# A transformer step on eight cores: softmax arithmetic reordered in every tile, and the first tile's weight loads, stores and constants rearranged

## The chip, the cores and the metric

The kernel runs on the eight cores of one Trainium2 chip, the same program on each core. The metric is the device time of the slowest core, in microseconds (us).

An execution falls into one of two states. In the fast one all cores agree within a fraction of a per cent. In the slow one cores of one die, or of both, get a lower TensorE clock for a part of the run or all of it, and the run is some per cent longer.

In the profiles PE is TensorE (PEld its weight loads), DVE is VectorE, ACT is ScalarE, POOL is GpSimd, and SP is SyncE, which here only issues transfers. L284 is line 284 of the kernel that ran; most operations go through helpers, so the same helper has another line number before and after.

## The reference

One encoder layer over 16 prompts of 4096 rows (65,536 rows of width 1024, so two prompts for each core), and over 16 short continuations of 16 rows (32 "sample rows" for each core):

```python
h = rms_norm(x, n_pre_mix)
q, k, v, zg, ga, gb = split(h @ w_in)
a = attn_prompt(q, k, v, sinks)          # 64-row chunks see themselves and two chunks before
u, gv = split(gelu(zg)); gv = layer_norm(gv, ln_g, ln_b)
bm = spatial_gate(u, gv, w_s, b_s)       # 128x128 lower-triangular mix
merged = sigmoid(ga) * (a @ w_attn_proj) + sigmoid(gb) * (bm @ w_gmlp_proj)
x = x + rms_norm(merged @ w_out, n_post_mix)
g, up = split(rms_norm(x, n_pre_ffn) @ w_ffn_in)
x = x + rms_norm((silu(g) * up) @ w_ffn_out, n_post_ffn)

# inside the attention: a softmax whose denominator has one more term for each head
denom = sum(p) + exp(sinks - m)
p = p / denom
```

Inputs, weights and outputs are f32.

## The kernel before

Each core works through 16 tiles of 512 rows; the 32 sample rows go along in tile 0. The weights are 34 blocks of up to 1 MB in bf16. They don't stay on the core: a ring of eight 1 MB slots is refilled all the time. In tile 0 a block is read as f32 by a converting DMA (on the POOL queue), in one, two or four pieces, and the bf16 result is stored to a scratch copy in HBM (on the SP queue). From tile 1 on, the SP queue reads the bf16 copy. This function keeps the ring filled:

```python
def pump():
    while W["issue"] < len(wseq) and W["free"]:
        ...                                        # next block `key`, slot s
        if key in W["seen"]:                       # later tiles: bf16 from scratch
            m.dma(SP, ("ring", s), ring[:, s, 0:nkc, :], view[key], reads=[("scr", key)], writes=RK(s))
            continue
        W["seen"].add(key)
        q = key[0] == "win" and key[1] < 2         # the two q blocks need a second slot
        g = W["free"].pop(0) if q else s
        for idx, src in f32_pieces(key):           # every piece writes RK(g): each waits for the last
            m.dma(POOL, ("ringc", g), ring[:, g][idx], src, writes=RK(g))
        if q:
            ...                                    # two DVE copies that lay the heads out anew
        m.dma(SP, ("cvst", key), view[key], ring[:, s, 0:nkc, :], reads=RK(s), writes=[("scr", key)])
```

Attention goes through eight pairs (of a 128-row block and two key heads) in a tile. `S(n)` makes the scores of pair n and their exponentials. `PV(n)` multiplies by the values (the first 256 columns of a bank) and by ones (the other 256, the sums), and ends with the division:

```python
def S(n):
    for c in range(2): ...      # score products on 64x128 tiles of the PE array
    for c in range(2): ...      # score products on 64x64 tiles
    act(PT[...], ..., AF.Exp); act(PT3[...], ..., AF.Exp)

def PV(n):
    ...                         # products with V (128x64, then 64x64) and with ones
    act(od, ps[:, 4:6, :], AF.Copy, B(4, 5), ok_)          # values and sums out of PSUM
    eng = DVE if FIRST[0] or n == 7 else POOL
    tt(eng, d4, d4, esb, ALU.add, ...)                     # + exp(sink)
    recip(od[:, :, 256:512], od[:, :, 256:512], ok_, ok_)  # on DVE
    tt(eng, ao, o4, d4, ALU.mult, ...)                     # into aT, bf16

for n in range(7):
    PV(n); S(n + 1); g_unit(2 * n + 2); g_unit(2 * n + 3)
    if n < 6: spatial(*sp[n + 2])
```

The start, and the sample rows' four rounds of attention at the end of mixing:

```python
for bl in range(4):                      # rows of x: statistics, scale, transpose
    ...
SM.load(); SM.norm(0)                    # sample rows
for u in qkv_units(tiles[0]): u()        # q, then k, then v
setup_rest()                             # gains, sinks, spatial weights: loads and preparation
SM.caches()
...
for n in range(4 if i0 else 0):          # at the end of tile 0's mixing
    SM.S(n); SM.PV(n)
```

The softmax here doesn't subtract the row's maximum and nothing guards it: scores larger than these inputs give would overflow.

Of the kernel before, what the change touches and what calls it, by code (L numbers as in the profile page):

```python
# [6 lines left out]
F32 = mybir.dt.float32  # L7
# [185 lines left out]
def build_program(n_prompt_tiles=16, do_sample=True):  # L193
# [34 lines left out]
    with ExitStack() as st:  # L228
# [18 lines left out]
        dent = sb("dent", [128, 2, 512], F32)  # L247
        hst = sb("hst", [128, 2, D], BF16)
        gvn = mgT.rearrange("p (s a) n -> p s (a n)", s=4)
# [24 lines left out]
        mgTs = sb("mgTs", [128, 8, 32], BF16)  # L274
        actTs = sb("actTs", [128, 22, 32], BF16)
        ps = st.enter_context(nc.psum_tensor("ps", [128, 8, 512], F32))
# [71 lines left out]
        FIRST = [True]  # L348
        PX = lambda: DVE if FIRST[0] else POOL

# [46 lines left out]
        wseq = list(QKV_KEYS)  # L397
# [7 lines left out]
        W = dict(issue=0, use=0, free=list(range(SLOTS)), where={}, seen=set())  # L405
# [3 lines left out]
        def pump():  # L409
            while W["issue"] < len(wseq) and W["free"]:  # L410
                u = W["issue"]
                key = wseq[u]
                s = W["free"].pop(0)
                W["where"][u] = s
                W["issue"] += 1
                nkc = view[key].shape[1]
                if key in W["seen"]:
                    m.dma(SP, ("ring", s), ring[:, s, 0:nkc, :], view[key], reads=[("scr", key)], writes=RK(s))
                    continue
                W["seen"].add(key)  # L420
                q = key[0] == "win" and key[1] < 2
                g = W["free"].pop(0) if q else s
                for idx, src in f32_pieces(key):
                    m.dma(POOL, ("ringc", g), ring[:, g][idx], src, writes=RK(g))
                if q:
                    d5 = ring[:, s].rearrange("p k (g h d) -> p k h g d", g=4, h=2)
                    s5 = ring[:, g].rearrange("p k (h g d) -> p k h g d", g=4, h=2)
                    for hh in range(2):
                        copy(DVE, d5[:, :, hh], s5[:, :, hh], RK(g), RK(s))
                    W["free"].append(g)  # L430
                m.dma(SP, ("cvst", key), view[key], ring[:, s, 0:nkc, :], reads=RK(s), writes=[("scr", key)])

        def wget(key):
            u = W["use"]
            assert wseq[u] == key, (u, wseq[u], key)
            pump()
            assert W["issue"] > u, ("no ring slot", key)
            W["use"] += 1
            s = W["where"].pop(u)
            return ring[:, s], ("ring", s), s  # L440
# [5 lines left out]
        def rsqrt(P, c, eps):  # L446

            o, i_ = stt[0:P, c + 1:c + 2], stt[0:P, c:c + 1]
            if FIRST[0]:
                ts(DVE, o, i_, float(eps), None, ALU.add, None, SK(c), SK(c + 1))  # L450
                act(o, o, AF.Sqrt, SK(c + 1), SK(c + 1))
                recip(o, o, SK(c + 1), SK(c + 1))
            else:
                ts(POOL, o, i_, float(eps), None, ALU.add, None, SK(c), SK(c + 1))
                tt(POOL, o, o, negh[0:P, 0:1], ALU.pow, SK(c + 1) + ["negh"], SK(c + 1))
# [17 lines left out]
        class PostNorm:  # L473
# [12 lines left out]
            def apply(self):  # L486
# [5 lines left out]
                if self.dst is None:  # L492
                    tt(DVE, self.x, self.x, tf, ALU.add, self.tk + self.xk, self.xk)
                else:
                    tt(PX(), tf, self.x, tf, ALU.add, self.tk + self.xk, self.tk)
                    q = ACT if FIRST[0] else POOL
                    m.dma(q, ("yst", self.ti, q), self.dst, tf, reads=self.tk)
# [9 lines left out]
        def scale_gamma(eng, i):  # L507
            ts(eng, gS[:, i, :], gS[:, i, :], 32.0, None, ALU.mult, None, [("gS", i)], [("gS", i)])

        load_gamma(0)  # L510
        m.op(POOL, lambda e: e.memset(negh[:], -0.5), writes=["negh"])
        m.op(POOL, lambda e: e.memset(ones[:], 1.0), writes=["ones"])
        t0_, t0k = tmp1()
        m.op(POOL, lambda e: e.memset(t0_[:, 0:128], 1.0), writes=t0k)
        m.op(POOL, lambda e: e.affine_select(out=t0_[:, 0:128], in_=t0_[:, 0:128], pattern=[[-1, 128]],
                                             compare_op=ALU.is_equal, fill=0.0, base=0, channel_multiplier=1),
             reads=t0k, writes=t0k)
        copy(DVE, ident[:], t0_[:, 0:128], t0k, ["ident"])
        scale_gamma(DVE, 0)
        pump()  # L520

        def setup_rest():
            for i in (1, 2, 3):
                load_gamma(i)
            m.dma(ACT, "c_lng", lng[:], ln_g[0:1, :].partition_broadcast(128), writes=["lng"])
            m.dma(ACT, "c_lnb", lnb[:], ln_b[0:1, :].partition_broadcast(128), writes=["lnb"])
            m.dma(ACT, "c_es", es[:], sinks[0:1, :].partition_broadcast(128), writes=["es"])
            for i in (1, 2, 3):
                scale_gamma(POOL, i)
            act(es[:], es[:], AF.Exp, ["es"], ["es"])  # L530
            for tp in range(2):
                for hf in range(2):
                    copy(DVE, es2[64 * hf:64 * hf + 64, 4 * tp:4 * tp + 4],
                         es[64 * hf:64 * hf + 64, 4 * (2 * tp + hf):4 * (2 * tp + hf) + 4], ["es"], ["es2"])
            a, ak = tmp1()
            wv = a.rearrange("p (g s) -> p g s", g=4)
            m.dma(ACT, "c_ws", wv, w_s.rearrange("g t s -> t g s"), writes=ak)
            m.op(POOL, lambda e: e.affine_select(out=wv, in_=wv, pattern=[[0, 4], [-1, 128]], compare_op=ALU.is_ge,
                                                 fill=0.0, base=0, channel_multiplier=1), reads=ak, writes=ak)
            wb = hst[:, 0, 0:512]  # L540
            copy(DVE, wb, a, ak, [("hst", 0)])
            for g in range(4):
                tp_(pTv[:, g * 128:(g + 1) * 128], wb[:, g * 128:(g + 1) * 128], ident[:], [("hst", 0)])
            copy(DVE, WmT[:].rearrange("p g t -> p (g t)"), pTv[:, 0:512], B(TB), ["WmT"])
            c, ck_ = tmp1()
            m.dma(ACT, "c_bs", c[0:1, :], b_s[0:1, :], writes=ck_)
            m.op(POOL, lambda e: e.memset(bsb[:], 0.0), writes=["bsb"])
            copy(DVE, bsb[0:1].rearrange("p g t -> p (g t)"), c[0:1, :], ck_ + ["bsb"], ["bsb"])
            if not do_sample:
                return  # L550
            d, dk = tmp1()
            wv2 = d[0:32, 0:128].rearrange("p (g s) -> p g s", g=4)
            m.op(POOL, lambda e: e.memset(d[0:32, 0:128], 0.0), writes=dk)
            for s in range(2):
                m.dma(ACT, "c_ws2", wv2[16 * s:16 * s + 16, :, 16 * s:16 * s + 16],
                      w_s[:, 0:16, 0:16].rearrange("g t s -> t g s"), writes=dk)
            m.op(POOL, lambda e: e.affine_select(out=wv2, in_=wv2, pattern=[[0, 4], [-1, 32]], compare_op=ALU.is_ge,
                                                 fill=0.0, base=0, channel_multiplier=1), reads=dk, writes=dk)
            wb2 = hst[0:32, 1, 0:128]
            copy(DVE, wb2, d[0:32, 0:128], dk, [("hst", 1)])  # L560
            for g in range(4):
                tp_(pTv[0:32, g * 32:(g + 1) * 32], wb2[:, g * 32:(g + 1) * 32], ident[0:32, 0:32], [("hst", 1)])
# [3 lines left out]
            m.op(POOL, lambda e: e.memset(msk[:], 1.0), writes=["msk"])  # L566
            for s, (base, cm) in enumerate(((15, -1), (-16, 1))):
                m.op(POOL, (lambda s, base, cm: lambda e: e.affine_select(
                    out=msk[:, s, :], in_=msk[:, s, :], pattern=[[0, 64]], compare_op=ALU.is_ge, fill=0.0, base=base,
                    channel_multiplier=cm))(s, base, cm), reads=["msk"], writes=["msk"])  # L570
# [12 lines left out]

        class Sample:
            KH = ["hTs"]
            x = gx[0:32, 1, :]
            XK = [("gx", 1)]

            def load(self):
                m.dma(ACT, "xs", self.x, xs[:, :], writes=self.XK)  # L590

            def norm(self, gi):
                r = nstats(32, self.x, self.XK, 0)
                nscale(32, self.x, self.XK, gi, r, 0)
                ntrans(32, 0, hTs[:], ["hTs"])
# [7 lines left out]
            def kv(self, w):  # L603
# [10 lines left out]
                for s in range(2):  # L614
                    m.dma(ACT, uniq("so"), ks[s, 112:128, :], t[16 * s:16 * s + 16, 0:256], reads=tk)
                    m.dma(ACT, uniq("so"), vs[s, 112:128, :], t[16 * s:16 * s + 16, 256:512], reads=tk)
                for src_c, dst_c in ((ck, ks), (cv, vs)):
                    m.dma(ACT, uniq("so"), dst_c[:, 0:112, :], src_c[:, 16:128, :])

            def caches(self):  # L620
                for s in range(2):
                    t, tk = tmp1()
                    m.dma(ACT, ("ckl", s), t[:, 0:256], ck[s], writes=tk)
                    m.dma(ACT, ("ckl", s), t[:, 256:512], cv[s], writes=tk)
                    copy(DVE, hst[:, s, 0:256], t[:, 0:256], tk, [("hst", s)])
                    copy(DVE, Vc[:, s, :], t[:, 256:512], tk, [("Vc", s)])
                    for j in range(2):
                        tp_(pTv[:, j * 128:(j + 1) * 128], hst[:, s, j * 128:(j + 1) * 128], ident[:], [("hst", s)])
# [666 lines left out]
```

## Time and profile before

| | before |
|---|---|
| first three runs | 4425.69, 4432.07, 5141.29 us (the last one slow) |
| profiled run, fast | 4423.02 us; spans of the cores 4407.2 to 4421.5, clock 0.976 to 0.979 |
| tile 0 with its start (median of the eight cores) | 545.7 us |
| a later tile | some 257.9 us (257 to 259), PE busy in 252.5 to 254 of them |

The slices, stretches and timelines (start, duration, engine, line, operation, and in brackets the idle time before it and what ended it) of this profile are quoted in the prediction. Each later tile begins with a load of the Gelu table on ACT, and I use the first such row after tile 0 as the end of tile 0. On the slowest core, core 3, in the timeline of ACT (start, duration, engine, line, operation, and in brackets the idle time before it and what ended it):

```profile
552.56 1.28 ACT L293 ACT_TABLE_LOAD   x1 [10.17 <-DMA ys<-gx]
```

PE's waits in the later tiles (view of waits, 1000 to 4200 us; columns: total us, times, longest) are led by the attention blocks and the spatial product:

```profile
PE ps L284 <- DVE aT L303: 24.6, 12, 2.1
PE ps L284 <- DVE big L303: 17.3, 26, 1.2
PE ps L284 <- POOL aT L303: 5.4, 12, 0.7
```

`aT` is the divided attention output: it comes late once a tile, by 2.1 us. `big` holds what the spatial products feed.

In tile 0 (the same core, 0 to 555 us) PE's three largest waits are far longer. The first is for copies of the constants and of the sample rows' caches (one of them 56.3 us), the second for normed rows, the third for banks that ACT frees:

```profile
PE ps L288 <- DVE hst L300: 71.5, 4, 56.3
PE ps L288 <- DVE hst L314: 62.1, 6, 29.9
PE ps L284 <- ACT big L293: 36.2, 4, 27.7
```

### The profile page before, as it was taken

The page shows a single profiled execution, that of the slowest core. Times are in us where ns is not written, and L with a number is a line of the kernel's source. Part 1 is how long each engine was busy: PE and PEld are TensorE (multiplying, and loading weights), DVE is VectorE, ACT ScalarE, POOL GpSimd, SP SyncE. Part 2 cuts the span into 40 slices and gives each one's busy share as a digit, 9 for nine tenths or more (in the row PEclk, how much of TensorE's full clock was granted, in tenths as well). Part 3 has the DMA queues.
Part 4 walks back from the last instruction along what each step waited for, and adds up shares of the span by engine and source line. Part 5 has one row for each costly group of instructions (what it writes and reads, how often), then busy time and mean ns, then how long its engine had stood idle before and what let it go on. Part 6 is the DMA issues. An engine that isn't in the chain of part 4 may idle for free.

```text
span 4421.5 us, 60878 instructions; the slowest of 8 cores (4407.2 to 4421.5 us)
## 1 busy us (share of the span) xinstructions
PE 4125.1 (93%) x23024; PEld 1929.8 (44%) x23024; DVE 1789.7 (40%) x1784; ACT 1386.2 (31%) x2151; POOL 802.2 (18%) x1023
## 2 busy tenths in 40 slices
PE   2569899999999999999999999999999999999988
PEld 1234344444444444444444444444444444444443
DVE  1343162443516244361634436162443616244351
ACT  1333142422414242241424224142422414242231
POOL 0101020302212030221203022120302212030211
PEclk9779999999999999999999999999999999999999
DMA  9659944545345454534545453454545345454532
GB/s 201 120 119 176 242 140 149 184 146 196 135 140 180 153 181 145 194 134 145 181 148 181 150 190 133 147 181 149 184 146 191 136 143 181 148 185 149 188 105 81
DMA packets 154876, 705.20 MB, mean 159 GB/s; under 512 B 13205, under 2 KB 59861, under 8 KB 89046
## 3 DMA queue, kind: packets, MB, share of 16 engines
q1 hardware_dynamic: 96192, 627.09, 41.3%
q0 software_dynamic: 55216, 67.12, 8.2%
q10 hardware_dynamic: 3182, 7.10, 0.6%
q8 instruction: 190, 3.11, 0.3%
q14 instruction: 96, 0.79, 0.1%
HBM read 666.85 MB, written 69.99 MB: 167 GB/s over the span
## 4 chain that ended last, share of the span: by engine, by line
PE 72%; DVE 10%; POOL 6%; DMA 5%; issue 4%; ACT 2%; ACTq 0%; another core or an unknown queue 0%; POOLq 0%; DVEq 0%; SPq 0%
PE ps L284 70%; DVE tmp L318 7%; POOL tmp L303 3%; POOL aT L303 2%; PE ps L288 1%; ACT tmp L293 1%; DMA yp<-tmp 1%; DVE tmp L314 1%; DMA ring<-wap 1%; DMA es<-sinks 1%; DVE hst L314 1%; DVE tmp L303 1%; POOL stt L303 1%; DMA ring<-w_in 1%; DMA ring<-wout 0%
## 5 line engine op out<-in xcount | busy, mean ns | idle before, releaser
L284 PE MATMUL ps<-aT,ring 128*128 128x512 bf16 x6656 | 1473.9, 381 | 36.2 <-DVE aT L303 28.7
L293 ACT ACTIVATE tmp<-ps 128x512 f32<-128x512 f32 (+2 forms) x620 | 475.5, 767 | 1835.8 <-PE ps L284 1660.3
L284 PE MATMUL ps<-hT,ring 128*128 128x512 bf16 x4352 | 999.9, 381 | 28.3 <-DVE big L303 20.9
L284 PEld LDWEIGHTS ps<-aT,ring 128*128 128x128 bf16 x6656 | 649.0, 98 | 817.2 <-issue 58.1
L303 DVE TENSOR_TENSOR big<-ps,tmp 128x512 bf16<-128x512 f32 x352 | 243.5, 692 | 985.3 <-PE ps L284 937.5
L284 PEld LDWEIGHTS ps<-hT,ring 128*128 128x128 bf16 x4352 | 410.9, 98 | 529.9 <-issue 58.3
L284 PE MATMUL ps<-ring,big 128*128 128x512 bf16 x2816 | 612.8, 380 | 8.2 <-DMA ring<-wfo 8.2
L307 POOL TENSOR_SCALAR stt<-stt 128x1 f32<-128x1 f32 x296 | 130.0, 439 | 2522.1 <-ACT tmp L293 2040.9
L318 DVE RECIPROCAL tmp<-tmp 128x512 f32<-128x512 f32 x128 | 429.2, 3353 | 244.4 <-POOL tmp L303 242.1
L314 DVE SCALAR_TENSOR_TENSOR tmp<-ps,stt,gS 128x1024 f32<-128x1024 f32 x129 | 165.6, 1284 | 766.0 <-POOL stt L303 732.5
L284 PEld LDWEIGHTS ps<-ring,big 128*128 128x128 bf16 x2816 | 275.4, 98 | 342.6 <-issue 12.4
L293 ACT ACTIVATE big<-ps 128x512 bf16<-128x512 f32 x384 | 229.6, 600 | 268.3 <-PE ps L284 268.3
L284 PE MATMUL ps<-ring,hT 128*128 128x512 bf16 (+1 forms) x1536 | 301.9, 349 | 7.5 <-DVE tmp L314 3.8
L284 PE MATMUL ps<-big,ring 128*128 128x512 bf16 x1024 | 237.2, 382 | 0.5 <-DVE tmp L314 0.5
L284 PE MATMUL ps<-ring,mgT 128*128 128x512 bf16 x1024 | 229.0, 379 | 2.0 <-DVE tmp L314 1.0
L288 PE MATMUL ps<-ident,hst 128*128 128x128 bf16 (+1 forms) x1052 | 87.2, 230 | 145.9 <-DVE hst L300 71.5
L284 PEld LDWEIGHTS ps<-ring,hT 128*128 128x128 bf16 x1536 | 150.3, 99 | 146.0 <-issue 20.7
L303 POOL TENSOR_TENSOR aT<-tmp 128x512 bf16<-128x512 f32 x105 | 144.8, 1379 | 378.5 <-DVE tmp L318 346.1
L293 ACT ACTIVATE PT<-ps 128x512 bf16<-128x512 f32 (+2 forms) x264 | 193.3, 790 | 13.8 <-PE ps L284 13.6
L314 DVE SCALAR_TENSOR_TENSOR tmp<-big,ps 128x1024 f32<-128x1024 bf16 x128 | 156.2, 1220 | 98.8 <-PE ps L284 97.8
L293 ACT ACTIVATE hT<-ps 128x1024 bf16<-128x1024 bf16 x64 | 65.6, 1025 | 395.3 <-PE ps L288 395.3
L303 POOL TENSOR_TENSOR stt<-stt,negh 128x1 f32<-128x1 f32 x296 | 170.6, 576 | 44.8 <-POOL stt L307 1.3
(125 smaller groups left out, 2559.8 us busy)
## 6 DMA issues: line engine op xcount, KB each, us to landing
ring<-s_win SPq DMA_DIRECT2D x165, 1024.0 KB, 5.5
ring<-s_wfi SPq DMA_DIRECT2D x165, 1024.0 KB, 5.3
ring<-s_wfo SPq DMA_DIRECT2D x60, 1024.0 KB, 5.5
xt<-xp SPq DMA_DIRECT2D x64, 512.0 KB, 5.1
gx<-xp SPq DMA_DIRECT2D x60, 512.0 KB, 5.4
ring<-s_wgp SPq DMA_DIRECT2D x30, 1024.0 KB, 12.7
ring<-s_wap SPq DMA_DIRECT2D x30, 1024.0 KB, 10.8
ring<-s_wout SPq DMA_DIRECT2D x30, 1024.0 KB, 5.0
```

Of the source, the lines that this page charges most:

```text
L284: m.op(PE, lambda e: e.matmul(out, lhsT=lhsT, rhs=rhs, start=start, stop=stop, skip_group_check=True), reads=reads, writes=[("ps", bank)])
L288: m.op(PE, lambda e: e.transpose(out=out, in_=in_, identity=idn), reads=reads + ["ident"], writes=[("ps", TB)])
L293: m.op(ACT, lambda e: e.activation(out=out, in_=in_, func=func, scale=scale, **kw), reads=reads, writes=writes)
L303: m.op(eng, lambda e: e.tensor_tensor(out=out, in0=in0, in1=in1, op=op), reads=reads, writes=writes)
L307: m.op(eng, lambda e: e.tensor_scalar(out=out, in0=in0, scalar1=s1, scalar2=None, op0=op0), reads=reads, writes=writes)
L314: m.op(DVE, lambda e: e.scalar_tensor_tensor(out=out, in0=in0, scalar=scalar, in1=in1, op0=op0, op1=op1), reads=reads, writes=writes)
L318: m.op(DVE, lambda e: e.reciprocal(out=out, in_=in_), reads=reads, writes=writes)
```

## The change

It has two aims. In every tile, POOL should not wait for DVE's reciprocal in place. In tile 0, loads, stores, constants and sample rows should not wait for one another in sequence. The core of the diff, cut:

```diff
 # every tile: the end of PV, and the order in S
-                eng = DVE if FIRST[0] or n == 7 else POOL
-                tt(eng, d4, d4, esb, ALU.add, ok_ + ["es2"], ok_)
+                tt(POOL, d4, d4, esb, ALU.add, ok_ + ["es2"], ok_)
+                if mults:
+                    mults.pop()(POOL)
                 recip(od[:, :, 256:512], od[:, :, 256:512], ok_, ok_)
-                tt(eng, ao, o4, d4, ALU.mult, ok_, [("aT", 4 * tp + g) for g in range(4)])
+                mults.append(lambda eng: tt(eng, ao, o4, d4, ALU.mult, ok_, [("aT", 4 * tp + g) for g in range(4)]))
+                if n == 7:
+                    mults.pop()(DVE)
 # (cut: in S the 64x64 score products now come before the 64x128 ones)

 # tile 0: stores spread over three tiles, pieces of a block not behind one another
+            if key not in STORE:
+                STORE[key] = 0 if key in QKV_KEYS else len(STORE) % 3
...
+                f32 = turn <= STORE[key]
...
-                for idx, src in f32_pieces(key):
-                    m.dma(POOL, ("ringc", g), ring[:, g][idx], src, writes=RK(g))
+                    for k, (idx, src) in enumerate(f32_pieces(key)):
+                        m.dma(POOL, ("ringc", g), ring[:, g][idx], src, writes=[] if k else RK(g))
 # (cut: the store is issued when the block is first used; k and v are projected before q)

 # tile 0: the start
+        first_stats(0)
+        first_stats(1)
+        pump(1)
+        first_stats(2)
+        first_rows(0)
+        first_stats(3)
+        pump(1)
...
+        pump()
+        const_loads()
         for u in qkv_units(tiles[0]):
             u()
-        setup_rest()
 # (cut: constants prepared among the gate projections; gains 1 to 3 loaded later; sample rows in
 #  buffers of their own, one attention round in place of four; outputs of tiles 0 to 2 stored by SP;
 #  the norms' and divisions' arithmetic of tile 0 on POOL, where before it was on DVE and ACT)
```

## The prediction

> **What bounds the kernel now.** I read the table of cores first (spans of 4407.2 to 4421.5 us, clocks of 0.976 to 0.979: no slow die), then the slices of the page, then busy times by stretch, then the instruction timeline of one later tile and of the start. The slices and the queue rows of the page:
>
> ```profile
> PE 4125.1 (93%) x23024; PEld 1929.8 (44%) x23024; DVE 1789.7 (40%) x1784; ACT 1386.2 (31%) x2151; POOL 802.2 (18%) x1023
> PE   2569899999999999999999999999999999999988
> PEclk9779999999999999999999999999999999999999
> DMA  9659944545345454534545453454545345454532
> ```
>
> A slice is 110.5 us. PE (TensorE) is the bound everywhere except in the first five slices. There, and only there, DMA is at 9 tenths, PE is low and the granted clock falls. So there are two questions: what the first tile of 512 rows costs, and what keeps a later tile from being PE alone. Busy time by stretch (us and instruction count of PE, PEld, DVE, ACT, POOL; then clock, DMA share, GB/s), tile 0 with its start first, two later tiles, then pieces of tile 0:
>
> ```profile
> 0.00:554.60 554.60, 353.82 (x2481) 174.08 (x2481) 169.90 (x262) 139.63 (x239) 54.33 (x69) 0.86 0.83 172
> 885.80:1143.70 257.90, 252.46 (x1384) 117.74 (x1384) 108.87 (x103) 84.22 (x129) 50.03 (x64) 1.00 0.47 162
> 2690.20:2948.10 257.90, 253.79 (x1385) 118.68 (x1384) 108.39 (x103) 84.09 (x129) 50.12 (x64) 0.99 0.46 161
> 93.00:160.00 67.00, 3.24 (x17) 1.60 (x18) 4.31 (x17) 1.50 (x2) 10.70 (x10) 0.50 0.80 176
> 235.00:320.00 85.00, 45.80 (x376) 23.88 (x375) 33.24 (x47) 25.19 (x43) 1.91 (x3) 0.72 0.47 116
> 400.00:447.00 47.00, 47.00 (x389) 23.91 (x388) 9.77 (x19) 8.52 (x18) 6.99 (x8) 1.00 1.04 195
> ```
>
> Tile 0 ends at 554.6 us; every later one takes 257.9 us, of which PE is busy some 253.3 and idle 4.6. From 93 to 160 us PE does nothing, and from 235 to 320 us both PE and DMA are half idle: tile 0 is not bound by one resource but by orders of waiting. From 400 to 447 us DMA is saturated (1.04). The rows that name the waits, from the timeline of the start:
>
> ```profile
> 58.08 9.48 PE L284 MATMUL ps<-hT,ring 128*128 128x512 bf16 x32
> 118.65 8.28 POOL L307 TENSOR_SCALAR gS<-gS 128x1024 f32<-128x1024 f32 x3 [32.00 <-DMA gS<-g]
> 132.23 1.28 ACT L293 ACT_TABLE_LOAD   x1 [55.80 <-DMA es<-sinks]
> 192.48 0.61 POOL L136 DMA_DIRECT2D ring<-wap  x1 [5.49 <-DMA ring<-wap]
> 320.14 0.87 POOL L136 DMA_DIRECT2D ring<-wfi  x1 [83.00 <-PE ps L284]
> ```
>
> The first projection starts only at 58 us. Then constants that mixing needs (gains, sinks, spatial weights) are fetched behind a full weight queue and hold ACT for 55.8 us. POOL issues the pieces of one weight block one after the other, each waiting for the last. And no weight load is issued for 83 us while PE works through sample rows.
>
> A later tile, its attention part:
>
> ```profile
> 2651.09 1.03 POOL L303 TENSOR_TENSOR tmp<-tmp,es 128x512 f32<-128x512 f32 x1
> 2652.23 3.35 DVE L318 RECIPROCAL tmp<-tmp 128x512 f32<-128x512 f32 x1 [1.96 <-POOL tmp L303]
> 2655.72 1.27 POOL L303 TENSOR_TENSOR aT<-tmp 128x512 bf16<-128x512 f32 x1 [3.60 <-DVE tmp L318]
> 2656.95 1.04 POOL L303 TENSOR_TENSOR tmp<-tmp,es 128x512 f32<-128x512 f32 x1
> 2680.64 1.89 PE L284 MATMUL ps<-hT,ring 128*128 128x512 bf16 x8 [1.16 <-DVE big L303]
> 2693.89 1.16 PE L284 MATMUL ps<-aT,ring 128*128 128x512 bf16 x4 [2.05 <-DVE aT L303]
> ```
>
> POOL adds, waits 3.60 us for DVE's reciprocal, multiplies, and only then adds for the next pair: a loop of 2656.95 - 2651.09 = 5.86 us. PE's work per pair is 5.46 us (it starts a pair's value product at 2648.08, 2653.54, 2659.00). So POOL's loop falls behind by 0.4 us a pair, and more where two statistics come between; PE then waits on the spatial product's bank (1.16 us) and at the end on the last attention block (2.05 us).
>
> **What the Trainium skill says.** "TensorEngine Tiling (Array Packing)", Tiling Modes, has that a change of tiling mode drains TensorE. The trace agrees: a gap of 0.20 us in weight loads at each change from 128x64 to 64x64 to 64x128 and back. "DMA: Bandwidth & Descriptors", SWDGE vs HWDGE vs iDMA, has that a cast during a DMA can only be issued from GpSimd; here all f32 weight loads are in fact on POOL, and all 1 MB bf16 stores and reloads on SP. "HBM Reference", Specifications, gives about 358 GB/s for each core where both of a pair stream. In the page's own counts (of 2-byte results) the first 100 us moved 196 GB/s at a share over 1; no run here shows the limit itself. "TensorE: Matmul & The Clock Gate", Part 1, has half clock after an idle window; the trace agrees (0.50 from 93 to 160 us).
>
> **The change, part by part.**
>
> (1) Later tiles. POOL's multiply for pair n-1 is put behind the add for pair n, so POOL no longer waits for the reciprocal in place; the last add goes from DVE to POOL. POOL then has 1.04 + 1.26 = 2.3 us per pair, and 3.2 us where a statistic comes between, DVE 3.35 + 0.63 = 4.0 us, ACT up to 5.0 us: all under PE's 5.46. For the end of attention, counted from the start T of the last value product: copy done at T+2.15, add at T+3.35, reciprocal T+6.8, multiply T+7.5. PE by then has 0.9 us of value product, 5.35 of gate product and 2.7 of the first half of the attention projection, so needs the block only at T+9.0. In the trace of before it came at T+11.3. So I expect the whole 4.6 us of idle time to go. Half of the score products are moved next to the value products of the same 64x64 mode: one drain fewer, about 0.12 us, times 7 = 0.85 us. The tiles at clock 0.99 are 1.3 us busier than those at 1.00; with no gaps some of that should go: 0.3 us. Sum 5.7 us a tile, times 15 = 86 us.
>
> (2) Tile 0. POOL's software queue no longer serializes pieces; each block's store to scratch is spread over tiles 0, 1 and 2 (14, 10 and 10 of 34 blocks), the others being read again in f32; constants are fetched before the projections; gains 1 to 3 later; k and v come first, which need one ring slot and no re-layout; sample rows are put among other work with their own buffers, and four sample attention rounds become one.
> PE's need: one steady tile's 253 us, 28 us for the first projections (58.08 to some 86 us in the trace), about 41 us for the remaining sample products (84 of 512 columns at 0.216 us, some 750 of 32 columns at 0.03 us) and 5 us of setup: 327 us. It can start when the rows are normed and the first block is in, about 22 us: 349 us.
> DMA's need, by packet times of the first 620 us: the software queue had 45.7% of 16 engines for 33.5 MB of results, 8.5 us for each MB; the SP queue 28.3% for 61.35 MB, 2.9 us. Tile 0: 33.5 x 8.5 + 14 x 2.9 + 9 (rows of x and three reloads) x 2.9 + 26 of constants = 378 us, at a share of 1.05 some 360 us. With 8 us before the first load, and the 25 us of PE work after the last block: 393 us. Before, the same sum had 20 more stores, 58 us, and gaps.
> Both limits are near one another, and early on PE waits for blocks. I take 392 us: 163 us less than 554.6.
>
> (3) Tile 1 pays for it: 20 blocks in f32, 14 in bf16, 10 stores, 6 MB of rows: 170 + 41 + 29 + 17 = 257 us, at 1.05 245 us, in a tile of 252. Tile 2: 85 + 70 + 29 + 17 = 201, at 1.05 191. The ring is 8 blocks ahead, and PE is slowest per block in attention, where DMA can catch up. I put the loss at 8 us in all.
>
> Sum: 4432 - 163 - 86 + 8 = 4191; as the DMA sum is on the heavy side (the queues' packets overlap), I say 4185 us.
>
> **The rivals.** First: DMA becomes the bound of tiles 0 and 1. For: the sums of 360 and 245 us, and that all eight cores read f32 at once. Against: blocks of w_in were loaded faster than the mean (11 issued by 86 us). It would make tile 0 430 us and tile 1 280 us: 4250. Second: POOL, in order, holds loads behind compute (or the other way) in tiles 0 to 2, where its loads wait for PE to free a slot; that is the 83 us wait in another place. For: POOL has loads and attention in one stream, and more of the norms' arithmetic now. Against: most waits are for PE work that comes before what follows on POOL. It would cost 20 to 40 us: 4215. Third: only the start gains, as PE's idle time in attention turns into another wait (the spatial bank on DVE, or banks on ACT, whose 5.0 us is close): then 4432 - 155 = 4277 or less. Fourth: tile 0 comes down to PE's 349 us and tile 1 loses nothing: 4140.
>
> **Range and chances.** 4135 to 4240 us, predicted 4185. Even with only half of part 2 and none of part 1 the gain is near 2%, so faster 0.97, same 0.02, slower 0.01.
>
> **What would show it.** Right: matmuls from about 22 us, the first later-type tile from about 390 us, POOL's wait on the reciprocal gone, tile period of 252 us from tile 3 on with PE idle under 1 us, DMA share over 0.9 in tile 1. Wrong: a period still over 255 us, with a wait of PE on a DVE or ACT row in attention; PE waits on "ring" loads in tile 1; POOL waits of tens of us ahead of a load in tile 0.

## The result

| fast runs | us |
|---|---|
| before, in the same rounds | 4420.56 to 4437.89, mean 4426.7 (11 of 15 runs fast) |
| after | 4181.66 to 4189.59 (5 of 12 runs fast) |
| ratio | 0.9453, 95% interval 0.944 to 0.9465 |

A ratio is the mean time of one kernel's fast runs over the mean of the other's fast runs of the same rounds, so it is not quite the ratio of the medians. The median over all twelve runs after is 4488.9 us, because seven of them were slow. The kernel is 5.5% faster, some 242 us.

The first profile of the changed kernel fell in the slow state on both dies, as the table of cores shows:

```profile
die 0 (median of its cores): 4965.1 us, clock 0.818
die 1 (median of its cores): 4996.5 us, clock 0.812
```

So I ran the same kernel again for a fast profile (the first experiment, 4195.66 us profiled and 4180.72 us). Its page, in the same slices as in the prediction (here of 104.8 us):

```profile
PE 4099.5 (98%) x23024; PEld 1930.2 (46%) x23024; DVE 1738.1 (41%) x1676; ACT 1359.6 (32%) x2100; POOL 897.9 (21%) x1156
...
PE   5999999999999999999999999999999999999988
PEclk7799999999999999999999999999999999999999
DMA  9799998774454544545454454544545454454532
```

PE has as many matmuls as before (23024), but is busy for 98% of a shorter span in place of 93%. Of the low slices of PE at the start only the first is left. DMA is at 7 tenths or more in all of the first nine slices, where before it dropped to 6 and 5 among the first five: the gaps are filled, and the stores and f32 reads reach on into tile 2.

The slowest core of this profile, core 6, was at a slightly lower clock (0.986), so for the stretches I take core 5 (0.992, span 4175.9 us). Columns as in the prediction: stretch, length, busy us and count of PE, PEld, DVE, ACT, POOL; clock, DMA share, GB/s. Tile 0, tile 1, tile 2 and a late tile:

```profile
0.00:394.70 394.70, 342.23 (x2463) 169.52 (x2464) 143.96 (x169) 109.74 (x186) 117.45 (x153) 0.95 0.98 178
394.70:646.10 251.40, 250.76 (x1386) 118.15 (x1384) 108.02 (x105) 87.18 (x133) 69.90 (x88) 1.00 0.99 207
646.10:897.50 251.40, 250.76 (x1385) 118.12 (x1384) 106.53 (x102) 84.37 (x129) 59.62 (x78) 1.00 0.81 207
2410.00:2661.90 251.90, 250.73 (x1385) 118.03 (x1384) 106.67 (x102) 83.99 (x131) 50.13 (x66) 1.00 0.49 165
```

Later tiles take 251.4 to 251.9 us where they took 257.9, with 0.6 to 1.2 us of idle PE where there were 4.1 to 5.4. Tile 1 is as short as tile 2, though its DMA share is 0.99. Tile 0 ends at 394.7:

```profile
394.66 1.28 ACT L296 ACT_TABLE_LOAD   x1 [4.49 <-DVE aT L306]
```

Over the eight cores the median end of tile 0 went from 545.7 to 396.2 us: 149.5 us. The rest of the span, from there to the end, went from 4412.3 - 545.7 = 3866.6 to 4176.6 - 396.2 = 3780.4 us (medians of the cores): 86.2 us, or 5.75 us for each of 15 tiles. Together 235.7 us. The split depends on the marker. PE starts the first Gelu product of tile 1 at 525.0 us before and 389.4 after (medians), 135.7 us apart; the rest of tile 0's gain then lies at the head of tile 1, which took 270.4 us from there before and 251.4 after. Where tiles of single runs are compared below, I go by this start of PE and say so.

The attention of a later tile after the change:

```profile
2190.81 1.04 POOL L306 TENSOR_TENSOR tmp<-tmp,es 128x512 f32<-128x512 f32 x1 [3.96 <-ACT tmp L296]
2191.81 1.27 POOL L306 TENSOR_TENSOR aT<-tmp 128x512 bf16<-128x512 f32 x1
2191.95 3.35 DVE L321 RECIPROCAL tmp<-tmp 128x512 f32<-128x512 f32 x1 [1.10 <-POOL tmp L306]
2193.85 0.41 PE L287 MATMUL ps<-PT,Vt 128*64 128x256 bf16 x4
2199.19 0.41 PE L287 MATMUL ps<-PT,Vt 128*64 128x256 bf16 x4
```

POOL now adds and multiplies back to back. It waits 3.96 us before the add, but for ACT's copy of the next pair, that is, for work that PE has just finished, and no longer for DVE. Pairs start 2199.19 - 2193.85 = 5.34 us apart.

The start shows what is left of tile 0's waiting. Stretches of core 5:

```profile
0.00:60.00 60.00, 33.87 (x240) 18.33 (x240) 14.86 (x20) 16.87 (x28) 16.86 (x33) 0.97 0.99 208
60.00:110.00 50.00, 28.03 (x131) 11.49 (x132) 14.10 (x28) 7.45 (x13) 5.54 (x8) 0.69 1.10 174
110.00:200.00 90.00, 85.63 (x772) 44.23 (x771) 56.80 (x48) 41.41 (x66) 43.95 (x48) 0.98 0.81 166
200.00:300.00 100.00, 100.00 (x719) 50.96 (x717) 40.28 (x50) 31.05 (x53) 30.03 (x43) 1.00 1.10 166
300.00:394.00 94.00, 94.00 (x603) 44.20 (x602) 17.79 (x25) 12.92 (x26) 21.06 (x23) 1.00 0.96 186
```

Of tile 0's 394.7 - 342.2 = 52.5 us without PE work, 26.1 lie before 60 us, 22.0 from 60 to 110 us, and 4.4 after that. In the middle stretch DMA is full. PE's waits on that core, tile 0 alone, name the blocks of `w_in` and the first rows:

```profile
PE ps L291 <- DVE big L317: 14.3, 1, 14.3
PE ps L287 <- DMA ring<-w_in: 13.5, 3, 7.7
PE ps L291 <- DVE hst L303: 7.8, 1, 7.8
```

The first of these is the wait for the first normed rows of x, at 14.27 us (they are written into a view of `big`); the last is the preparation of the constants, at 94.8 us, which still costs 7.8 us.

### The profile page after: what moved, and what is told of

It is laid out like the page before. It is cut to its first block, busy times and chain, and to the rows that moved or that the text cites. A ratio compares the mean times of both kernels' runs of the same rounds, so it can differ in the third digit from the quotient of the medians.

```text
span 5008.3 us, 60608 instructions; the slowest of 8 cores (4961.0 to 5008.3 us)
## 1 busy us (share of the span) xinstructions
PE 4925.4 (98%) x23024; PEld 2139.7 (43%) x23024; DVE 1742.6 (35%) x1676; ACT 1380.0 (28%) x2100; POOL 901.2 (18%) x1156
## 4 chain that ended last, share of the span: by engine, by line
PE 96%; DMA 1%; ACT 1%; DVE 1%; POOL 1%; issue 0%; another core or an unknown queue 0%; POOLq 0%; DVEq 0%; ACTq 0%; SPq 0%
PE ps L287 95%; PE ps L291 1%; DMA ring<-w_in 1%; ACT hT L296 0%; DVE tmp L317 0%; ACT big L296 0%; POOL tmp L306 0%; DMA xt<-xp 0%; DMA gs<-aT 0%; POOL stt L306 0%; POOL stt L310 0%; DVE stt L773 0%; DVE xt L306 0%; ACT tmp L296 0%
## 5 line engine op out<-in xcount | busy, mean ns | idle before, releaser
L287 PE MATMUL ps<-aT,ring 128*128 128x512 bf16 x6656 | 1776.2, 437 | 1.3 <-ACT aT L296 1.3
L287 PE MATMUL ps<-hT,ring 128*128 128x512 bf16 x4352 | 1200.7, 439 | 11.1 <-DVE ring L303 5.3
L287 PEld LDWEIGHTS ps<-aT,ring 128*128 128x128 bf16 x6656 | 721.6, 109 | 1006.5 <-issue 1005.9
L287 PEld LDWEIGHTS ps<-hT,ring 128*128 128x128 bf16 x4352 | 459.4, 109 | 664.4 <-issue 664.0
L287 PE MATMUL ps<-ring,big 128*128 128x512 bf16 x2816 | 742.4, 436 | 0.0
L310 POOL TENSOR_SCALAR stt<-stt 128x1 f32<-128x1 f32 x325 | 153.7, 473 | 2996.6 <-ACT tmp L296 2327.4
L287 PE MATMUL ps<-ring,hT 128*128 128x512 bf16 (+1 forms) x1536 | 356.1, 395 | 7.4 <-DMA ring<-w_in 7.4
L287 PE MATMUL ps<-ring,mgT 128*128 128x512 bf16 x1024 | 277.0, 436 | 0.4 <-DVE mgT L306 0.4
L306 POOL TENSOR_TENSOR tmp<-tmp,es 128x512 f32<-128x512 f32 x128 | 132.7, 1037 | 491.7 <-ACT tmp L296 485.2
L296 ACT ACTIVATE PT<-ps 128x512 bf16<-128x512 f32 (+1 forms) x258 | 192.5, 804 | 0.2
L287 PEld LDWEIGHTS ps<-ring,mgT 128*128 128x128 bf16 x1024 | 111.3, 109 | 158.1 <-issue 157.8
```

Of the source, the lines that this page charges most:

```text
L287: m.op(PE, lambda e: e.matmul(out, lhsT=lhsT, rhs=rhs, start=start, stop=stop, skip_group_check=True), reads=reads, writes=[("ps", bank)])
L296: m.op(ACT, lambda e: e.activation(out=out, in_=in_, func=func, scale=scale, **kw), reads=reads, writes=writes)
L306: m.op(eng, lambda e: e.tensor_tensor(out=out, in0=in0, in1=in1, op=op), reads=reads, writes=writes)
L310: m.op(eng, lambda e: e.tensor_scalar(out=out, in0=in0, scalar1=s1, scalar2=None, op0=op0), reads=reads, writes=writes)
```

## The experiments

The twelve runs asked three things: whether both halves of the change give what the prediction's sum says, which step inside each half does it, and whether something better lies near. All twelve gave correct results. Times are fast runs unless said otherwise.

**1. The changed kernel again.** No edit.

> The changed kernel once more, to get a profile in the fast state. Fast runs of 4180 to 4190 us (it had 4181.66 to 4189.59). By the prediction's steps: first projection near 22 us, tile 1 starts near 392 us, later tiles 252 us apart with PE idle under 1 us each, tile 1 and 2 together 8 us longer than later ones. Rival (tile 0 is bound by DMA): tile 1 starts near 430 us and later tiles are shorter than 252 us to make up for it. Rival (tile 0 at PE's own 349 us): tile 1 starts near 350 us and later tiles are longer than 252 us.

Measured: 4195.66 and 4180.72 us, two more runs slow. The first is 6 us over the expected range, with cores 6 and 7 at clocks of 0.986 and 0.987. Its profile is the one shown above. In both slow runs one die stayed at clocks of 0.986 to 0.994, with 4171 to 4199 us a core, while the other fell to 0.93 to 0.97: the changed kernel itself is repeatable.

**2. The attention part alone, on the kernel before.**

```diff
-                eng = DVE if FIRST[0] or n == 7 else POOL
+                eng = DVE if FIRST[0] else POOL
                 tt(eng, d4, d4, esb, ALU.add, ...)
+                if mults:
+                    mults.pop()(eng)
                 recip(...)
-                tt(eng, ao, o4, d4, ALU.mult, ...)
+                mults.append(lambda eng: tt(eng, ao, o4, d4, ALU.mult, ...))
+                if n == 7 or FIRST[0]:
+                    mults.pop()(DVE)
 # and the 64x64 score products before the 64x128 ones
```

> The kernel before with the attention part alone in tiles 1 to 15: the multiply of a pair behind the add of the next one, the last add on POOL, and the 64x64 score products first (these in tile 0 too). My theory: 86 us less than before, so about 4342 us, ratio 0.9805, tile period 252 us, tile 0 unchanged at some 554 us. Rival (the wait turns into another one): less than 40 us gained, with PE waiting in attention on a DVE or ACT row.

Measured: 4335.02 us; a second run at 4393.88 us lies 1.4% higher, so I lean on the first, and on the profile's undisturbed die, whose cores took 4313.5 to 4322.7 us at clock 0.980 (before: 4407.5 to 4417.4). Against a before of 4423.2 us in the same rounds, or 4411.6 us for the die, the gain is 88 to 92 us. The tile period is 251.7 us, as in the full change. So the attention part alone brings what the later tiles gain; run 6 takes it apart.

**3. The start alone, on the changed kernel.** The end of PV and the score order put back, all else kept:

```diff
-                tt(POOL, d4, d4, esb, ALU.add, ...)
-                if mults:
-                    mults.pop()(POOL)
+                eng = DVE if TILE[0] == 0 or n == 7 else POOL
+                tt(eng, d4, d4, esb, ALU.add, ...)
                 recip(...)
-                mults.append(...)
+                tt(eng, ao, o4, d4, ALU.mult, ...)
```

> The changed kernel with the attention part as before (multiply right behind its reciprocal, last add on DVE, 128-row score products first): only the start is new. My theory of two parts that add up: about 4185 + 86 = 4270 us, later tiles 257.9 us apart, tile 0 as in the changed kernel. If the two parts help one another (the longer PE waits hid loads, or the loads on POOL lengthen POOL's loop in tiles 1 and 2) the sum of the two single gains will differ from the gain of both by over 15 us.

Measured: 4269.5 and 4281.84 us (mean 4275.7, some 148 below before). Tile 0 ends at 391.6 to 399.3 us, as in the whole change, although its attention arithmetic is on DVE here; tile 1 takes 258 us. 88 for the attention (run 2) and about 148 for the start make 236; the whole change gave about 242. The halves add up, and neither hides the other.

**4. Every store in tile 0.**

```diff
-                STORE[key] = 0 if key in QKV_KEYS else len(STORE) % 3
+                STORE[key] = 0
```

> The changed kernel with every block's store to scratch in tile 0, so no block is read in f32 twice. 20 more stores of 1 MB in tile 0 at 2.9 us are 58 us of packet time; tiles 1 and 2 lose 8.5 us each for 30 f32 reads and 20 stores. If DMA bounds tile 0 (the sum of 360 us), it becomes some 50 us longer and tiles 1 and 2 up to 8 us shorter: 4225 us. If PE bounds tile 0 (349 us) and DMA had slack, under 15 us are lost: 4185 to 4200 us.

Measured: 4218.2, 4229.95 and 4235.53 us (mean 4227.9), 43 above the changed kernel; in the last two some cores were at clocks of 0.980 to 0.985. In the profile (the first run) tile 0 takes some 32 us more on the median of the cores, tile 1 its 251.4, and the median span is 4206.8 us against 4176.6. The stretches (same columns) and the wait of PE that takes the time:

```profile
200.00:340.00 140.00, 137.02 (x1075) 71.15 (x1089) 52.44 (x69) 38.26 (x70) 36.40 (x52) 1.00 1.16 218
340.00:439.00 99.00, 68.96 (x306) 29.05 (x313) 10.58 (x11) 7.03 (x13) 13.29 (x14) 0.86 0.86 208
```

```profile
PE ps L287 <- DMA ring<-wfo: 27.9, 5, 8.8
```

DMA runs over full up to 340 us, and then PE is busy for only 69 of 99 us, waiting for the last blocks. So spreading the stores is worth 30 to 43 us. Twenty more stores at the prediction's 2.9 us make 58 us of packet time, of which some 32 came out as time of tile 0.

**5. The score order alone, on the kernel before.** Only the two loops of `S` change places.

> The kernel before with only the order of the score products changed: the 64x64 ones first, next to the value products of the same mode. My theory: one drain of about 0.12 us saved 7 times in each of 16 tiles, 13 us, so about 4411 us, ratio 0.997. But in attention of the kernel before PE waits anyway for POOL's loop of 5.86 us a pair; PE time saved inside that loop is then no gain. By that rival: 0 to 3 us, ratio 0.9995 to 1.000, the gap between modes gone but PE's wait longer by as much. The gain then shows only together with the other attention change.

All timed runs fell in the slow state. The profile has one undisturbed die (its cores 4409.0 to 4423.4 us; before 4407.5 to 4417.4):

```profile
die 1 (median of its cores): 4415.8 us, clock 0.977
```

Core 5 of it, PE's waits from 1000 to 4200 us and a tile:

```profile
PE ps L284 <- DVE big L303: 24.9, 38, 1.3
PE ps L284 <- DVE aT L303: 24.6, 12, 2.1
```

```profile
2125.10:2383.30 258.20, 253.40 (x1382) 118.36 (x1381) 108.46 (x102) 83.96 (x130) 49.15 (x63) 0.99 0.45 160
```

The drain saved does not shorten the tile while POOL's loop sets the pace: the wait on `big` grows from 17.3 to 24.9 us instead.

**6. The deferred multiply alone, on the kernel before.** As in 2, without the exchange in `S`.

> The kernel before with only the multiply put behind the next pair's add and the last add on POOL, score products in the old order. Both parts together gained about 86 us (4335.0 against 4421.4). If the drain is worth its 13 us once POOL's loop is gone: about 4348 us, tile period 252.7 us. If the drain is worth nothing: 4335 us, tile period 251.8 us.

Measured: 4357.51, 4353.04 and 4348.94 us, ratio to before 0.9835 (0.9819 to 0.9851), so some 73 us. Against run 2's 88 to 92 that leaves 15 to 19 us for the score order, where alone it gave nothing. The timeline of PE here, two value products of consecutive pairs:

```profile
2113.74 0.41 PE L284 MATMUL ps<-PT,Vt 128*64 128x256 bf16 x4
2119.19 0.41 PE L284 MATMUL ps<-PT,Vt 128*64 128x256 bf16 x4
```

A pair takes 5.45 us; with the new order it takes 5.34 (shown above). 0.11 to 0.12 us a pair, seven or eight pairs a tile, 15 tiles: 12 to 14 us. That is the size of the drain, and with the loop out of the way most of the difference between the runs is this.

**7 and 8. Stores moved to later tiles,** to take DMA work out of the stretch where PE still waits (60 to 110 us):

```diff
-                STORE[key] = 0 if key in QKV_KEYS else len(STORE) % 3
+                k = len(STORE)
+                STORE[key] = 0 if key in QKV_KEYS else 1 + k % 2 if key[0] == "win" else (0, 0, 1, 2)[k % 4]
```

(run 8: 1 in place of the first 0).

> The changed kernel with none of the eight blocks of w_in that tile 0 needs first after q, k, v stored in tile 0; as many stores are made in tile 0 as before (14), but of later blocks. In the changed kernel PE lost some 52 us in the first 100 us of tile 0 and hardly anything after; DMA was at share 1.1 there. Three stores of 2.9 us fewer there: if the early blocks bound the start, 6 to 9 us gained (4175 us). If tile 0 is bound by the sum of DMA over the tile, nothing is gained, as the sum is the same.

> As the run before, and the three q, k, v blocks are stored at their second use, late in tile 0, so they are read in f32 twice (three f32 reads of about 5.6 us more in packet time than a reload) and nothing at all is stored in the first 60 us. If the early blocks bound the start: another 6 to 9 us gained (4167 us). If the extra reads in the output projection of tile 0 make PE wait for the feed-forward's blocks: as much is lost there, and 4175 to 4185 us come out.

Both missed. Measured: 4206.81 to 4217.39 us (ratio 0.9513) and 4212.68 to 4216.51 us (0.9522): some 25 to 30 us slower than the changed kernel. Run 7 by stretch:

```profile
60.00:110.00 50.00, 30.84 (x152) 13.11 (x153) 15.52 (x29) 9.18 (x15) 6.65 (x10) 0.76 1.12 165
386.00:658.00 272.00, 256.20 (x1386) 119.35 (x1386) 108.37 (x104) 85.13 (x130) 69.94 (x87) 0.97 0.95 197
658.00:922.00 264.00, 255.10 (x1386) 119.24 (x1385) 108.89 (x102) 85.18 (x131) 56.74 (x74) 0.98 0.73 199
```

The last two are tiles 1 and 2 on core 5, by PE's start; PE's largest wait in tile 1:

```profile
PE ps L287 <- DMA ring<-w_in: 15.0, 3, 9.2
```

The early stretch did gain: 30.8 us of PE work in place of 28.0, and by PE's start tile 0 ends 3 us sooner (386.0 us, median). But tile 1 takes 269 us and tile 2 263 on the median of the cores (251.4 each in the changed kernel), at DMA shares no higher than there (0.95 and 0.73, against 0.99 and 0.81). In tile 1 PE waits for `w_in` at its head: with this rule all eight `w_in` blocks that follow one another there are f32 reads. I read this as a matter of how many f32 reads come in a row, not of how many the tile has; the changed kernel's rule mixes the two kinds. A run that changes the order alone was not made, so this is not shown. In tile 2 PE waits for no block, but 6.8 us for DVE in attention: at 709.9 us POOL issues a load for which it has waited 13.0 us, until the store out of that ring slot had landed, and the add of an attention pair stands behind it. Run 10 shows the same on a larger scale.

**9. Thirty-one blocks read in f32 three times,** stores all in tile 2:

```diff
+                STORE[key] = 0 if key in QKV_KEYS else 2
```

> The changed kernel with all blocks but q, k, v read in f32 in tiles 0, 1 and 2 and stored in tile 2: the cost of DMA in tiles 1 and 2 raised until it must show. By the prediction's packet times tile 1 needs 31 x 8.5 + 3 x 2.9 + 17 = 289 us and tile 2 31 x 11.4 + 26 = 379 us; at the share of 1.1 that was seen, 263 and 345 us, against 251.4 of PE: 12 and 94 us longer. Tile 0 has 11 stores fewer: by the run with 20 more stores (35 us) it gains up to 19 us if DMA is its bound, and nothing if its early blocks are. Sum 4270 to 4290 us. If packet times overstate what a block costs: 4200 to 4250 us.

Measured: 4275.08 and 4278.98 us, as forecast. By stretch, on core 0, tile 1 and tile 2 by PE's start:

```profile
393.30:644.40 251.10, 248.90 (x1357) 117.96 (x1383) 106.77 (x102) 83.54 (x128) 84.50 (x106) 1.00 1.08 161
644.40:984.80 340.40, 270.83 (x1359) 121.70 (x1384) 107.93 (x102) 84.89 (x131) 83.93 (x106) 0.89 1.06 218
```

Two things follow. Tile 0 got no shorter (by ACT's marker a median end of 394 us, against 396) though it has 11 stores fewer than the changed kernel: there, DMA's sum is no longer what sets the end. Tile 1, with a DMA sum forecast at 263 us, took 251.4 on the median of the cores and lost nothing: the sum by packet times is a few per cent heavy, or the ring's eight blocks of lead carried the rest into tile 2. And tile 2, with nearly all f32 reads and all stores, is bound by DMA: on the median of the cores 337 us, for a sum of 345.

**10. Pieces of a block one after the other again.**

```diff
-                        m.dma(POOL, ("ringc", g), ring[:, g][idx], src, writes=[] if k else RK(g))
+                        m.dma(POOL, ("ringc", g), ring[:, g][idx], src, writes=RK(g))
```

> The changed kernel with each piece of a weight block waiting for the last one again (4 pieces for the attention projection's blocks, 2 for the feed-forward's), as before the change, in all tiles that read f32. In the kernel before a feed-forward block took 11.3 us at that, with its store, at a share of 1.04: saturated in spite of the waits. If that is so here, under 10 us are lost. If POOL's waits between pieces keep DMA from being filled, tile 0 and tile 1 each lose 20 us or more, with POOL waits on its own loads: over 4220 us.

The first branch missed by far; the second (over 4220 us, POOL waiting on its own loads) came true, at a size that I had not expected. Measured: 4359.24 and 4355.85 us, 173 us above the changed kernel. By PE's start (medians of the cores) tile 0 ends 77 us later, tile 1 takes 309 us and tile 2, which still reads ten blocks in f32, 288, where both take 251.4 in the changed kernel. DMA shares are low, here on core 3:

```profile
0.00:470.60 470.60, 341.49 (x2432) 168.50 (x2432) 139.99 (x166) 109.08 (x183) 111.98 (x148) 0.89 0.82 147
470.60:780.80 310.20, 256.06 (x1386) 119.39 (x1386) 108.56 (x104) 84.33 (x129) 71.06 (x89) 0.92 0.78 168
780.80:1073.30 292.50, 256.44 (x1385) 119.92 (x1384) 106.93 (x101) 84.38 (x129) 59.04 (x78) 0.93 0.70 178
```

So DMA was not short of capacity. Nor did PE wait longer for weights: for `w_in` 14.4 us in tile 0 (13.5 in the changed kernel), and for no block in tiles 1 and 2. The timeline of POOL shows why, with what DVE and PE did at the same time:

```profile
140.15 0.61 POOL L136 DMA_DIRECT2D ring<-wap  x1 [14.47 <-DMA ring<-wap]
...
166.01 0.61 POOL L136 DMA_DIRECT2D ring<-wap  x1 [13.24 <-DMA ring<-wap]
...
175.99 0.61 POOL L136 DMA_DIRECT2D ring<-wap  x1 [4.49 <-DMA ring<-wap]
176.62 1.05 POOL L306 TENSOR_TENSOR tmp<-tmp,es 128x512 f32<-128x512 f32 x1
```

```profile
177.77 3.35 DVE L321 RECIPROCAL tmp<-tmp 128x512 f32<-128x512 f32 x1 [42.61 <-POOL tmp L306]
```

```profile
181.82 3.27 PE L287 MATMUL ps<-hT,ring 128*128 128x512 bf16 x8 [39.11 <-DVE big L306]
```

POOL takes its instructions in order. The issue of the second piece of a block waits for the first piece to land, and so on; the add of the first attention pair stands behind these issues; the reciprocal waits 42.6 us for that add; PE waits 39.1 us for a bank that DVE reads only after the reciprocal. In tiles 1 and 2 PE's longest waits, 34.5 and 28.5 us, are again for DVE in attention. In the kernel before, the pieces were serial too, but tile 0's attention arithmetic was on DVE, out of POOL's stream, and tiles 1 and 2 read no block in f32. By the trace it is the meeting of the two in POOL's stream that costs; serial pieces with the arithmetic back on DVE were not run. Run 3 shows the other corner: with independent pieces tile 0 ends no later when its attention arithmetic is on DVE, so moving that to POOL gained nothing by itself.

**11. No wait of the first load for the second block of rows.**

```diff
-        m.fence([POOL], XK(1))
         pump(1)
```

> The changed kernel without POOL's wait for the second block of rows before its first weight load, so that weights are asked for at about 4 us and not 11 us. If the first 100 us are bound by the weights' loads, up to 6 us are gained (4177 us); if the rows come later by as much because they share DMA with the weights, nothing or a few us are lost. A candidate for a better version.

Measured: 4177.23, 4184.25 and 4184.34 us, mean 4181.9; the changed kernel 4184.4. Its first projection starts at 25.1 us, where the fast profile of the changed kernel has 27.4 on its slowest core and 27.2 on core 5, but the busy time of PE up to 110 us is the same (33.3 + 28.3 us, against 33.9 + 28.0 on core 5). The gain, if there is one, is within the noise; what limits PE there comes later, in the loads.

**12. Constants loaded after the first projections.**

```diff
         pump()
-        const_loads()
         for u in qkv_units(tiles[0]):
             u()
+        const_loads()
```

> The changed kernel with the constants (sinks, layer norm gains, spatial weights, caches) asked for after the first projections, as before the change, in place of ahead of them. In the kernel before, ACT waited 55.8 us for them. If that wait was due to the place alone, 20 to 40 us are lost here (4205 to 4225 us), with ACT or DVE waiting on a constant's load. If it was due to what stood behind them (everything else waited for them in turn, and here they are used later), under 8 us are lost, or some are gained as early weights come sooner.

Measured: 4183.86 to 4187.73 us (four runs, mean 4186.5): some 2 us lost, at the edge of the noise. Before, the wait that ended with the sinks' load was 55.8 us. So moving these loads ahead of the projections is not what removed it. The traces show what differs: before, the sinks were asked for at 93.2 us and took 39.0 us to land, and the spatial weights were asked for only at 132.3 us, behind ACT's wait for the sinks; in run 12 the two were asked for at 58.9 and 61.6 us, the sinks landed in 9.6 us, and PE's wait for the constants was 13.6 us on core 1 (7.8 in the changed kernel, 71.5 before). What made the landing faster (no store and no serial piece in front, or the later gains) was not separated.

## Why the prediction was right, point by point

*The total.* 4185 us was predicted (the sum of 4191, less 6 for a DMA sum held to be heavy); the fast runs after are 4182 to 4190 us. The start of the sum, 4432, was a median with a slow run in it; fast runs before are at 4421 to 4438, mean 4426.7.

*Later tiles, 86 us.* Measured from the end of tile 0 on: 86.2 us, in which the prediction's loss of 8 us in tiles 1 and 2 is already counted, so 78 was forecast for this stretch. The working held in its parts: POOL's wait on the reciprocal is gone, the period is 251.4 to 251.9 us (252 forecast), PE idles 0.6 to 1.2 us (under 1 forecast). The drain of 0.12 us a pair came out as 5.45 to 5.34 us; runs 5 and 6 show that it counts only with the loop gone. The third rival (PE's idle time becomes another wait) fell with run 2. It did hold for one step alone, the score order in run 5.

*Tile 0, 163 us saved, an end at 392.* Measured: 149.5 us on the median of the cores, and an end at 396.2. Most of the difference lies in the starting point: the prediction took 554.6 us from the slowest core, where the median is 545.7. From the latest core before to the latest core at full clock after it is 552.6 - 398.9 = 153.7. The number is right, but the account of it is only half right. The prediction had two limits, PE's 349 us and DMA's 393, and took the second. PE's busy time was 342 us (327 forecast, 15 too low; the granted clock was 0.95 in tile 0, and how much of the 15 us is due to that was not separated), and the first projection began at 27.4 us (22 forecast). PE's idle time lies almost wholly before 110 us: the wait for the first rows and block, then for `w_in` at a DMA share of 1.1, and for the constants; after that PE is full. A sum over the whole tile does not see that. Run 4 shows that the DMA sum is close behind (20 stores more, some 32 us more), run 9 that it is not the limit (11 stores fewer, nothing gained).

*Tile 1, 8 us lost.* Measured: nothing; tile 1 and tile 2 take 251.4 us each, at DMA shares of 0.99 and 0.81. This term was mis-sized: runs 7 and 9 show that such losses exist (269 us in tile 1 with all of `w_in` in f32, 337 in tile 2 with nearly every block), but here it was nil. The 8 us too many here and the 9 to 14 us too few in tile 0 nearly cancel, which is luck.

*The rivals.* DMA as the bound of tiles 0 and 1 (4250) fell; with every store in tile 0 it would have come near (run 4, 4228). POOL's loads ahead of its arithmetic (4215) did not happen in the changed kernel, where PE has no long wait after 110 us; but run 10 shows that the mechanism is there and far larger than the 20 to 40 us that the prediction gave it: 173 us over three tiles. What keeps it away in the changed kernel is a single edit, pieces without mutual waits; run 7 shows a small case of it without serial pieces. PE's bare 349 us (4140) was not reached because of the first 110 us.

*What stays open.* The start is a bundle. Shown: the spread of stores is worth 30 to 43 us (run 4), the independent pieces are worth 173 us with the arithmetic on POOL, 77 of them in tile 0 (run 10), the constants' place some 2 us (run 12). The traces name more: PE's wait for the constants fell from 71.5 to 7.8 us, and its wait for the first normed rows from 29.9 to 14.3. Not separated: how much the sample rows' own buffers and single round give, which removed the 83 us without a weight load of the kernel before, and how much the order k, v, q gives. These steps were not undone one by one, so how the 149 us divide among them is not shown.

## What to carry to other kernels

When an engine works on chained steps with another, put the next item's first step ahead of this item's last one, and check the sum of both engines' work against the bound engine's period. Before an engine that issues DMAs gets arithmetic on the critical path, look at what its issues wait for: here one that waited for data to land held back the arithmetic behind it. Extra DMA work was better spread over several stages here, and what counts is the stage where it runs out of slack, not the sum over a tile.

## What the runs showed of the hardware that I had not expected

- Serial issue of the pieces cost 173 us here, though DMA was at a share of only 0.82: in tile 0 the longest single waits of DVE and PE were for arithmetic that stood behind the issues (a reciprocal held up for 42.6 us).
- A DMA share near 1 need not cost time: tile 1 ran at 0.99 and took 251.4 us like tile 2 at 0.81. In run 9 even a share of 1.08 gave a tile of 251 us.
- The slow state took both dies to a clock of 0.81 while PE stayed fully busy, so that a tile took 304.0 us at 303.5 us of PE work; in fast runs the same work at the same density held 0.99 on all eight cores. No run here tells what decides between them. It need not hold for a whole run or die: in run 5's profile cores 0 and 1 took 257 to 259 us a tile for the first tiles after tile 0, at clocks of 0.98 to 1.00, and 303 to 305 us from some 2400 us on, at 0.81; cores 2 and 3 of the same die took some 304 us up to 2700 us and 257 to 259 after some 2990.

```profile
480.00:784.00 304.00, 303.47 (x1385) 131.48 (x1384) 106.66 (x101) 85.40 (x130) 70.25 (x88) 0.81 0.78 174
```

## What the Trainium skill lacked or had wrong

- "TensorEngine Tiling (Array Packing)", Tiling Modes, says that a change of mode drains the array, without a price. Here one change fewer in a pair of attention blocks was worth 0.11 to 0.12 us (5.45 to 5.34 us a pair), and nothing while another engine set the pace (run 5).
- "TensorE: Matmul & The Clock Gate", Part 1, gives 13/16 of the clock (81%) once three cores of a die run dense matmuls. The slow profile agrees in the number (0.812 and 0.818), the fast one does not: 0.990 and 0.993 on the two dies, with PE busy for 97 to 98% of the span on all eight cores.
- I found on no page what a converting weight load costs. Here it was 8.5 us of packet time for each MB of bf16 result, against 2.9 us for a plain transfer; sums from these came out a few per cent heavy (run 9: 263 us forecast for tile 1, 251.4 measured; 345 and 337 for tile 2).
- "Perfetto Trace Analysis", Tensor Engine Instruction, calls GPSIMD a strict FIFO, and run 10 agrees. I found on no page what follows for DMA issues on it: one that waits for an earlier transfer holds back the arithmetic behind it, here up to 14.5 us for one piece, and 173 us on 4184 for run 10 as a whole.
